# Attention softmax, gate, transposes and masks of a hybrid decoder layer: sinks as a 129th key slot, a tanh gate, turns two blocks behind, weights scaled on ScalarE, masks by affine selection

## The chip, the cores and the metric

One Trainium2 chip, one core of it. The metric is the device time of one execution of the whole program, in microseconds (us), the median of several runs. The engines are named as the profile names them: PE (TensorE matmul), PEld (its weight load), DVE (VectorE), ACT (ScalarE), POOL (GpSimd) and SP (SyncE, which issues the DMAs here). Each engine works through its own instruction list in order.

## What is computed

One decoder layer over 2048 tokens of width 1024, in float32. Batch is 1, depth is 1.

```python
hn = rms_norm(h, ln1_g); proj = hn @ w_in + b_in          # q 512 | k 128 | v 128 | u 512
q, k = partial_rotary(q), partial_rotary(k)
s = q k^T / 8 within a window of 128, 8 heads over 2 key-value heads
m = max(max(s), sink); p = exp(s - m)
attn = (p / (sum(p) + exp(sink - m))) @ v
y = gelu(s5_ssm(u, ...))                                   # tanh form of gelu
ssm = y * sigmoid(y @ w_glu + b_glu)
h = h + concat(rms_norm(attn, g_attn), rms_norm(ssm, g_ssm)) @ w_out
up = causal_conv3(rms_norm(h, ln2_g) @ w_up) + conv_b      # 2 x 2816 columns
h = h + (silu(gate) * val) @ w_down
out = rms_norm(h, lnf_g)
```

`rms_norm(x, g)` is `x * rsqrt(mean(x * x) + 1e-5) * g`.

## The kernel before

Nearly every product is made of three matmuls in the rounded format `F32R`: a number is split in a high half (a cast on ACT) and a low half (the subtraction on DVE or POOL), and high by high, high by low and low by high are summed in PSUM. The helper `split` (L133 and L115) records that. `tt_` (L115), `stt_` (L118) and `ts_` (L112) are helpers through which most elementwise work goes, so their line numbers mix many places, and the tile names tell them apart. The program runs under a scheduler that places each instruction in its engine's list and interleaves independent work, so the order of the lists is not that of the source.

The work falls into stretches of the timeline:

1. **Projection** (0 to 292 us). Blocks of 128 tokens are normalised, turned by PE, split and multiplied by `w_in`. Beside it DVE, POOL and ACT build the tables of the state space model. `rstd_of` (L119 to 129) gives the reciprocal root of a mean square: one `pow` on POOL and a Newton step on DVE.
2. **Attention beside the state space model** (292 to 616 us). `attention(b)` (L678) handles block b, for each of the two key-value heads four query heads at once: scores on PE (L695), the previous block's 128 keys copied by ACT (L699) and overwritten under a triangular mask by the block's own keys (L700), so that one tile `s` of 128 queries by 4 heads by 128 key slots holds each window. Then the maximum (L704), the negated maximum with the sink (`m`, by `stt_`), the sink's own term `e` (an addition and an exponential, L707), four exponentials with sums (L709), the sum with `e`, the reciprocal (L711) and the product of weights and reciprocal, 128x512, on DVE. PE turns the weights (L715), they are split into `th` and `tl`, POOL multiplies both by a mask into `mh` and `ml`, and PE multiplies by values (L735). `ssm(j)` runs between the blocks, and `attn_out` (L832) multiplies a finished block by the upper half of `w_out`.
3. **Gate, lower half of the output and turns** (616 to 842 us, with the start of the next). For every quarter q of 256 tokens: `d_gelu(q)` (L871) loads and applies gelu (L877); `d_gate(q)` (L883) multiplies by `w_glu` (L891) and applies the sigmoid (L893); `d_out(q, t)` (L941) multiplies a block of 128 tokens by the lower half of `w_out` (L804), adds, squares on ACT (L953) and normalises into `hn`; `d_turn(b)` (L958) turns `hn` by eight PE transposes (L965), copies them out by ACT (L966) and stores them. The loop at L1107 sets the order of these calls. ACT loads a table when the function it is to compute is not in the table it holds (ACT_TABLE_LOAD).
4. **Convolution and feed-forward** (842 us to the end): five passes of a seven-product scheme (`pair`, L1060, L1077), with elementwise work on all engines, and the final norm.

The loop that sets the order in stretch 3 is, in the kernel before:

```python
        d_out(q, 0)
        if q + 2 < NQ:
            d_gelu(q + 2)
        if q > 0:
            d_turn(q * 2 - 1)
        d_out(q, 1)
        d_turn(q * 2)
```

Of the kernel before, what the change touches and what calls it, by code (L numbers as in the profile page):

```python
# [68 lines left out]
def trunk(ctx, tc, a, out):  # L69
# [610 lines left out]
    def attention(b):  # L680
# [5 lines left out]
        for kv in range(NKV):  # L686

            s = xa.tile([P, 4, P], F32, name="u_t", bufs=4) if early else ap_.tile([P, 4, P], F32, name="s", bufs=4)
            if b == 0:
# [12 lines left out]
            e = sm.tile([P, 4], F32, name="e")  # L702
# [1 line left out]
            V.tensor_reduce(out=m, in_=s, axis=AX.X, op=ALU.max)  # L704
            stt_(m, m, -1.0, nsink[:, kv * 4:kv * 4 + 4], ALU.mult, ALU.min)
            tt_(e, sink[:, kv * 4:kv * 4 + 4], m, ALU.add)
            S.activation(out=e, in_=e, func=AF.Exp)  # L707
            for h in range(4):
                S.activation(out=s[:, h], in_=s[:, h], func=AF.Exp, bias=m[:, h:h + 1], accum_out=den[:, h:h + 1])  # L709
            tt_(den, den, e, ALU.add)  # L710
# [1 line left out]
            tt_(s, s, den.rearrange("p (h o) -> p h o", o=1).broadcast_to([P, 4, P]), ALU.mult)
# [581 lines left out]
```

## Time and profile before

| | |
|---|---|
| median of 3 runs | 2155.77 us (2153.46 to 2157.44) |
| the profiled execution, its own time | 2155.07 us |
| its span, first to last instruction | 2152.9 us |
| mean granted TensorE clock | 0.975 of full |
| PE, PEld busy | 93%, 78% of the span |
| DVE, ACT, POOL busy | 78%, 47%, 58% |

Busy time of PE is the union of matmuls that overlap in the pipeline, so a stretch in which PE is 90% busy can hold more idle issue slots than 10%. The shares over the whole span mix stretches with different limits; the section of rows below has them apart. The time outside the span (2.2 us) is the start and end of the execution.

### The profile page before, as it was taken

What the parts mean: (1) busy time and instruction counts of PE and PEld (TensorE: products, weight loads), DVE (VectorE), ACT (ScalarE), POOL (GpSimd) and SP (SyncE); (2) the same over time, 40 slices, a digit from 0 to 9 for tenths busy, and PEclk for the clock granted to TensorE, in tenths of its full rate; (3) what the DMA queues carried; (4) which work ended last, traced back from release to release, by engine and by line L of the source; (5) the groups of instructions that cost most, each with busy time, mean ns of one, the idle gap of its engine ahead of it and who ended that gap; (6) DMA issues with size and microseconds to landing.
All of it is one profiled execution on the core that took longest, in us unless ns stands there. A gap on an engine that the chain in (4) does not pass through costs nothing.

```text
span 2152.9 us, 29873 instructions
## 1 busy us (share of the span) xinstructions
PE 2003.9 (93%) x10057; PEld 1681.7 (78%) x10057; DVE 1681.9 (78%) x2778; ACT 1013.6 (47%) x2071; POOL 1238.0 (58%) x1180
## 2 busy tenths in 40 slices
PE   7999987899889988999999999999999899999986
PEld 6889976788778867888888778888887687788664
DVE  6988357999976787777777987877779967857888
ACT  5575335655546644444444554444544423323333
POOL 1656215666642355555555775454547868968864
PEclk9999987999999999999999999999999999999998
DMA  7476478677746752313233323132333545645543
GB/s 211 147 270 245 140 244 248 200 225 233 198 147 196 227 194 92 104 60 98 79 113 102 118 88 108 60 98 79 108 100 124 208 150 192 219 162 169 198 149 130
DMA packets 304622, 335.50 MB, mean 156 GB/s; under 512 B 92070, under 2 KB 237910, under 8 KB 302934
## 3 DMA queue, kind: packets, MB, share of 16 engines
q1 hardware_dynamic: 304470, 333.60, 48.2%
q8 instruction: 80, 1.31, 0.2%
q14 instruction: 72, 0.59, 0.1%
HBM read 214.14 MB, written 119.41 MB: 155 GB/s over the span
## 4 chain that ended last, share of the span: by engine, by line
PE 48%; DVE 8%; POOL 4%; issue 2%; DMA 2%; ACT 1%; DVEq 0%; ACTq 0%; POOLq 0%
PE ps L1077 17%; PE pz L1077 17%; PE pi L1077 7%; PE po L1077 6%; DMA sg<-in_w_down_dram 1%; DVE sums L115 1%; DVE yl L115 1%; DVE sg L115 1%; DVE yl L118 1%; DVE rs L118 1%; POOL xt L115 1%; POOL ln L115 1%; DVE rs L115 1%; PE pi L804 0%; PE po L804 0%
## 5 line engine op out<-in xcount | busy, mean ns | idle before, releaser
L118 DVE SCALAR_TENSOR_TENSOR pp<-yl,cw,pp 128x512 f32<-128x512 f32 x176 | 131.9, 750 | 38.5 <-ACT pp L1158 37.9
L115 POOL TENSOR_TENSOR rs<-rs,mhalf 128x1 f32<-128x1 f32 x80 | 51.6, 652 | 162.7 <-DVE rs L112 156.3
L1163 ACT ACTIVATE xh<-pp 128x512 f32<-128x512 f32 x88 | 52.7, 598 | 93.9 <-DVE pp L118 93.0
L1158 ACT ACTIVATE pp<-yl,cb,cw 128x512 f32<-128x512 f32 x88 | 69.0, 784 | 53.9 <-DVE yl L115 52.9
L115 DVE TENSOR_TENSOR yl<-pz,yl 128x512 f32<-128x512 f32 x66 | 45.3, 686 | 49.6 <-PE pz L1077 47.2
L115 POOL TENSOR_TENSOR xt<-sums,xt 128x512 fp32r<-128x512 f32 (+1 forms) x39 | 52.6, 1349 | 48.1 <-ACT xt L133 48.1
L218 PE MATMUL pz<-hnT_lo,wu_h 128*128 128x256 f32 x256 | 73.6, 290 | 2.6 <-DVE hnT_lo L115 2.6
L115 POOL TENSOR_TENSOR atl<-sums,atl 128x512 fp32r<-128x512 f32 (+1 forms) x40 | 56.2, 1404 | 33.2 <-ACT atl L133 33.1
L218 PE MATMUL pz<-hnT_hi,wu_h 128*128 128x256 f32 x256 | 71.9, 290 | 3.2 <-ACT hnT_hi L133 3.2
L115 POOL TENSOR_TENSOR ln<-sums,ln 128x512 fp32r<-128x512 f32 (+1 forms) x43 | 55.8, 1299 | 31.5 <-ACT ln L133 30.9
L218 PE MATMUL pz<-hnT_hi,wu_l 128*128 128x256 f32 x256 | 72.5, 286 | 0.0
L115 POOL TENSOR_TENSOR sq<-sums,sq 128x512 fp32r<-128x512 f32 (+1 forms) x42 | 54.7, 1303 | 27.6 <-ACT sq L133 26.0
L115 DVE TENSOR_TENSOR sums<-yt 128x512 f32<-128x512 f32 (+1 forms) x48 | 59.4, 1238 | 13.6 <-POOL ln L115 4.0
L115 POOL TENSOR_TENSOR ath<-sums,ath 128x512 fp32r<-128x512 f32 (+1 forms) x40 | 55.2, 1380 | 25.4 <-ACT ath L133 25.4
L709 ACT ACTIVATE s<-s,m 128x128 f32<-128x128 f32 x120 | 46.9, 392 | 43.2 <-DVE m L118 43.2
L115 POOL TENSOR_TENSOR sq<-sq 128x256 f32<-128x256 f32 (+1 forms) x64 | 42.7, 680 | 42.0 <-ACT sq L817 39.6
L115 POOL TENSOR_TENSOR vv<-vv 128x255 f32<-128x255 f32 x32 | 26.3, 822 | 67.6 <-DVE vv L115 62.6
L115 DVE TENSOR_TENSOR sg<-sg,sg 128x2048 f32<-128x2048 f32 (+1 forms) x20 | 51.5, 2575 | 15.5 <-DMA sg<-in_w_down_dram 11.0
L804 PE MATMUL pi<-w_oh,ath 128*128 128x512 f32 x128 | 55.0, 430 | 8.6 <-DVE rs L112 6.2
L115 DVE TENSOR_TENSOR xh<-px,xh 128x512 f32<-128x512 f32 x88 | 60.5, 687 | 1.9
L115 POOL TENSOR_TENSOR xt<-yh,xt 128x512 fp32r<-128x512 f32 (+1 forms) x28 | 41.5, 1480 | 28.5 <-ACT xt L133 28.4
L115 DVE TENSOR_TENSOR yl<-ps,yl 128x512 f32<-128x512 f32 x70 | 47.9, 685 | 11.3 <-PE ps L1077 10.0
(1261 smaller groups left out, 7966.9 us busy)
## 6 DMA issues: line engine op xcount, KB each, us to landing
xh<-h_d SPq DMA_DIRECT2D x48, 512.0 KB, 4.1
yt<-in_w_up_dram SPq DMA_DIRECT2D x44, 512.0 KB, 4.2
yh<-in_w_up_dram SPq DMA_DIRECT2D x44, 512.0 KB, 3.8
act_d<-xh SPq DMA_DIRECT2D x44, 512.0 KB, 3.3
h_d<-yl SPq DMA_DIRECT2D x32, 512.0 KB, 3.7
qk_d<-qx SPq DMA_DIRECT2D x16, 768.0 KB, 3.2
sg<-h_d SPq DMA_DIRECT2D x12, 1024.0 KB, 6.0
sg<-in_w_down_dram SPq DMA_DIRECT2D x12, 1024.0 KB, 5.7
```

Of the source, the lines that this page charges most:

```text
L115: (eng or V).tensor_tensor(out=o, in0=x, in1=y, op=op)
L118: V.scalar_tensor_tensor(out=o, in0=x, scalar=s, in1=y, op0=o0, op1=o1)
L218: E.matmul(out=pu, lhsT=l["u"][:, k, cs], rhs=r[:, k, :], start=n == 0, stop=n == 3 * KT - 1)
L709: S.activation(out=s[:, h], in_=s[:, h], func=AF.Exp, bias=m[:, h:h + 1], accum_out=den[:, h:h + 1])
L804: E.matmul(out=po, lhsT=l[:, k, :], rhs=r[k][:, cs], start=n == 0, stop=n == 11)
L1077: E.matmul(out=b, lhsT=l[:, k], rhs=r[:, k], start=m == 0, stop=m == 3 * kh - 1)
L1158: S.activation(out=v, in_=u[s_][:, o + 2:o + 2 + HF], func=AF.Identity, scale=w2, bias=cb[:, fc_:fc_ + 1])
L1163: S.activation(out=x, in_=v, func=AF.Silu)
```

## The change

- `rstd_of` takes two DVE operations behind the `pow` and not three. It gives minus two times the value, and the factor is taken back in the gains: `ln1`, `g_a`, `g_s`, `ln2` and `lnf` are scaled once when they are loaded, and `sumsq` gets a scale for the gated half.
- In `attention` for all blocks but the first, the sink is a 129th column of two fixed tiles (`slots`, one for even and one for odd blocks, each with both key-value heads), filled once by POOL. Maximum and exponentials run over 129 columns; `m`, `e`, their addition and the addition to the sum go away. The exponentials write to a tile `w`.
- The weights are multiplied by the reciprocal in four ACT operations of 128x128 (Copy with a scale per partition), not in one of DVE.
- `mh` and `ml` are made by affine selection on POOL, and not by a product with a mask.
- The gate is `tanh(x/2) + 1` times gelu, with the factors taken into `bg` and `g_s`; the multiplication becomes a `stt_`.
- `d_gelu`'s load is a function of its own, `d_load`, called a quarter earlier.
- `d_turn` runs two blocks behind `d_out`, and `hn` of every first block of a quarter stands in a `sums` tile.

```diff
@@ rstd_of
-        tt_(t, y, y, ALU.mult)
-        stt_(t, t, -0.5, v, ALU.mult, ALU.mult)
-        stt_(r, t, 1.5, y, ALU.add, ALU.mult)
+        stt_(t, y, v, y, ALU.mult, ALU.mult)
+        stt_(r, t, -3.0, y, ALU.add, ALU.mult)
@@ attention
+            else:
+                s = slots[b % 2]
...
-            V.tensor_reduce(out=m, in_=s, axis=AX.X, op=ALU.max)
-            stt_(m, m, -1.0, nsink[:, kv * 4:kv * 4 + 4], ALU.mult, ALU.min)
-            tt_(e, sink[:, kv * 4:kv * 4 + 4], m, ALU.add)
-            S.activation(out=e, in_=e, func=AF.Exp)
...
+                s = s[:, kv]
+                V.tensor_reduce(out=m, in_=s, axis=AX.X, op=ALU.max, negate=True)
+                w = ap_.tile([P, 4, P + 1], F32, name="w")
             for h in range(4):
-                S.activation(out=s[:, h], in_=s[:, h], func=AF.Exp, bias=m[:, h:h + 1], accum_out=den[:, h:h + 1])
-            tt_(den, den, e, ALU.add)
+                S.activation(out=w[:, h], in_=s[:, h], func=AF.Exp, bias=m[:, h:h + 1], accum_out=den[:, h:h + 1])
             V.reciprocal(out=den, in_=den)
-            tt_(s, s, den.rearrange("p (h o) -> p h o", o=1).broadcast_to([P, 4, P]), ALU.mult)
+                for h in range(4):
+                    S.activation(out=w[:, h, 0:P], in_=w[:, h, 0:P], func=AF.Copy, scale=den[:, h:h + 1])
...
-                tt_(mh, f(th), kb_(cc[:, C_MC:C_MC + P], 4), ALU.mult, Q)
-                tt_(ml, f(tl), kb_(cc[:, C_MC:C_MC + P], 4), ALU.mult, Q)
+                for o, i in ((mh, th), (ml, tl)):
+                    Q.affine_select(out=o, in_=i, compare_op=ALU.is_ge, fill=0.0, base=0,
+                                    pattern=[[0, 4], [1, P]], channel_multiplier=-1)
@@ d_gate
-            S.activation(out=pg, in_=pg, func=AF.Sigmoid, bias=bg[:, o:o + 1])
-            tt_(sm_[:, o].rearrange("p k t -> p t k"), yg[:, o].rearrange("p (t k) -> p t k", t=T),
-                pg.rearrange("p (t k) -> p t k", t=T), ALU.mult)
+            S.activation(out=pg, in_=pg, func=AF.Tanh, bias=bg[:, o:o + 1], scale=0.5)
+            stt_(sm_[:, o].rearrange("p k t -> p t k"), pg.rearrange("p (t k) -> p t k", t=T), 1.0,
+                 yg[:, o].rearrange("p (t k) -> p t k", t=T), ALU.add, ALU.mult)
@@ d_out
-        hn = xh()
+        hn = xh() if t else acc.tile([P, D], F32, name="sums", bufs=2)
@@ the loop over quarters
+        if q + 3 < NQ:
+            d_load(q + 3)
         d_out(q, 0)
         if q + 2 < NQ:
             d_gelu(q + 2)
         if q > 0:
+            d_turn(q * 2 - 2)
+        d_out(q, 1)
+        if q > 0:
             d_turn(q * 2 - 1)
-        d_out(q, 1)
-        d_turn(q * 2)
```

DVE's list, in the middle of the attention stretch, for about one key-value head: `zb` is the scan of the state space model, `xh` the sum of an output block, `rs` the rstd. Before, and then in the changed kernel:

```order
L704 TENSOR_REDUCE m<-s 128x4
L115 TENSOR_TENSOR ul<-u,uh 128x512
L115 TENSOR_TENSOR tl<-pp,th 128x512
L118 SCALAR_TENSOR_TENSOR m<-m,aux 128x4
L700 COPY_PREDICATED s<-cc,ps 128x256
L115 TENSOR_TENSOR e<-aux,m 128x4
L118 SCALAR_TENSOR_TENSOR xh<-pi,rs,xh 128x512
L115 TENSOR_TENSOR den<-den,e 128x4
L711 RECIPROCAL den<-den 128x4
L115 TENSOR_TENSOR s<-s,den 128x512
```

```order
L704 COPY_PREDICATED s_3991<-cc,ps 128x2x128
L118 SCALAR_TENSOR_TENSOR rs<-rs 128x1
L716 TENSOR_REDUCE m<-s_3991 128x4
L722 RECIPROCAL den<-den 128x4
L118 SCALAR_TENSOR_TENSOR xh<-pi,rs,xh 128x512
L115 TENSOR_TENSOR zl<-vv,zh 128x512
L627 SCALAR_TENSOR_TENSOR zb_3460<-rad,vv 128x255
```

Four DVE operations for each head pair are gone, three of them small and one of 128x512; between maximum and reciprocal only other work is left.

ACT's list in the same stretch, before and then changed (`u` is the output of the state space model, `th` the split of the turned weights):

```order
L699 COPY s<-ps 128x256
L709 ACTIVATE s,den<-s,m 128x128 x4
L707 ACTIVATE e<-e 128x4
L133 CAST th<-pp 128x512
L699 COPY s<-ps 128x256
```

```order
L719 ACTIVATE w,den<-s_3991,m 128x129 x4
L640 COPY u<-pz 128x256
L727 ACTIVATE w<-w,den 128x128 x4
L703 COPY s_3991<-ps 128x2x128
L132 CAST ath<-po 128x512
```

Four scalings (L727) stand behind the four exponentials, and what is behind them on ACT waits while DVE takes the reciprocal.

ACT's list in the stretch of gates and turns, before and then changed (`yt` is gelu, `pz` the gate, `xh` or `sums` the square of an output block, `xt` the copies of a turn):

```order
L953 ACTIVATE xh,ss<-yl 128x1024
L877 ACT_TABLE_LOAD
L877 ACTIVATE yt<-yt 128x1024
L893 ACT_TABLE_LOAD
L893 ACTIVATE pz<-pz,bg 128x256
L966 COPY xt<-pp 128x512
L966 COPY xt<-px 128x512
```

```order
L986 ACTIVATE xh,ss<-yl 128x1024
L922 ACTIVATE pz<-pz,bg 128x256 x2
L906 ACTIVATE yt<-yt 128x1024
L922 ACTIVATE pz<-pz,bg 128x256
L132 CAST yh<-yt 128x1024
L922 ACTIVATE pz<-pz,bg 128x256
L999 COPY xt<-pp 128x512
```

The table loads around gelu and gate are gone: the whole program has 16 before and 5 now, two of the five in front of a gelu and one of them in front of an exponential of the last blocks.

## Rows read from the trace of the kernel before

**Rows 1.** Windows: length, then busy (count) PE PEld DVE ACT POOL, PEclk, DMA, GB/s.

```profile
292.00:360.00 68.00, 46.36 (x242) 40.42 (x241) 53.44 (x106) 35.03 (x89) 28.47 (x26) 0.75 0.85 262
360.00:616.00 256.00, 230.21 (x1502) 206.03 (x1502) 237.68 (x492) 148.04 (x471) 161.17 (x152) 0.96 0.68 206
616.00:700.00 84.00, 81.34 (x498) 71.76 (x497) 55.81 (x118) 48.97 (x76) 21.39 (x34) 1.00 0.65 189
700.00:842.00 142.00, 122.99 (x628) 103.44 (x627) 102.26 (x169) 73.13 (x117) 68.94 (x68) 0.94 0.60 188
842.00:2130.00 1288.00, 1245.68 (x5342) 1006.59 (x5341) 1014.88 (x1326) 546.20 (x896) 823.32 (x672) 0.99 0.38 125
```

**Rows 2.** The chain (start, length, work), then PE's timeline: matmuls 512 and 256 wide.

```profile
869.68 2.80 PE ps L1077 x12
...
690.20 0.28 PE L891 MATMUL pz<-yh,uwl 128*128 128x256 f32 x1
690.32 0.40 PE L891 MATMUL pz<-yh,uwh 128*128 128x256 f32 x2
690.55 0.28 PE L891 MATMUL pz<-yh,uwl 128*128 128x256 f32 x1
```

**Rows 3.** Windows of L804 alone, PE and PEld: its 512-wide matmuls in 360 to 616.

```profile
360.00:616.00 256.00, 89.74 (x338) 65.59 (x338) 0.96 0.68 206
```

**Rows 4.** Waits of PE, 616 to 842: us, times, longest; then a window of 8 us.

```profile
PE pp L965 <- DVE xh L118: 10.7, 4, 5.4
...
PE pp L965 <- DVE rs L118: 2.2, 1, 2.2
PE pz L891 <- DVE sm__9239 L115: 2.2, 1, 2.2
...
756.00:764.00 8.00, 5.82 (x26) 5.09 (x25) 7.96 (x8) 2.56 (x5) 4.76 (x3) 0.57 0.36 126
```

**Rows 5.** Groups of DVE, 360 to 616: count, busy, mean ns, idle before.

```profile
L115 DVE TENSOR_TENSOR s<-s,den 128x512 f32<-128x512 f32 x28 | 26.4, 942 | 0.1
...
L115 DVE TENSOR_TENSOR den<-den,e 128x4 f32<-128x4 f32 x28 | 13.2, 473 | 3.0 <-ACT e L707 2.5 <-ACT s L709 0.4
L115 DVE TENSOR_TENSOR e<-aux,m 128x4 f32<-128x4 f32 x28 | 12.1, 431 | 0.1
L118 DVE SCALAR_TENSOR_TENSOR m<-m,aux 128x4 f32<-128x4 f32 x28 | 10.2, 365 | 0.0
...
L115 DVE TENSOR_TENSOR rs<-rs 128x1 f32<-128x1 f32 x14 | 5.8, 412 | 0.5 <-POOL rs L115 0.4
```

**Rows 6.** L115 on DVE in 360 to 616: ns min/median/max; then the timeline.

```profile
L115 DVE TENSOR_TENSOR e<-aux,m x28: 127/162/1247, 362.9 to 596.1; 128x4 f32<-128x4 f32 x28
...
L115 DVE TENSOR_TENSOR s<-s,den x28: 660/688/1771, 367.2 to 598.8; 128x512 f32<-128x512 f32 x28
...
341.50 2.35 POOL L115 TENSOR_TENSOR w_ol<-xh,w_oh 128x1024 fp32r<-128x1024 f32 x1
...
341.82 2.05 DVE L115 TENSOR_TENSOR e<-aux,m 128x4 f32<-128x4 f32 x1
```

**Rows 7.** Groups of ACT by form, 90 to 180: scale per partition, 128x128.

```profile
L513 ACT ACTIVATE tt<-tb,php 128x128 f32<-128x128 f32 x16 | 6.3, 396 | 4.3 <-DVE tb L118 4.1
```

**Rows 8.** POOL: the masks of 360 to 616; a cast of one input (ns min/median/max).

```profile
L115 POOL TENSOR_TENSOR mh<-th,cc 128x512 fp32r<-128x512 f32 x29 | 40.3, 1388 | 25.0 <-ACT th L133 24.9
...
L169 POOL CAST wu_h<-u_t x1: 697/697/697, 11.1 to 11.1; 128x512 fp32r<-128x512 f32 x1
```

**Rows 9.** Groups of ACT, 616 to 842: table loads; then one in the timeline.

```profile
L893 ACT ACT_TABLE_LOAD x7 | 9.0, 1283 | 0.1
L877 ACT ACT_TABLE_LOAD x6 | 7.7, 1283 | 14.3 <-DMA yt<-ys_d 14.3
...
839.93 1.28 ACT L1163 ACT_TABLE_LOAD   x1
841.23 0.60 ACT L1163 ACTIVATE xh<-pp 128x512 f32<-128x512 f32 x1
```

More of the change, by code (lines that the diff above doesn't have):

```diff
@@ L177, in trunk @@
     Y.dma_start(out=ln1, in_=a["ln1_g"][0].rearrange("(k p) -> p k", p=P))
+    S.mul(out=ln1, in_=ln1, mul=-0.5)
     load_w("u", 0)
@@ L686, in attention @@
         for kv in range(NKV):
-            s = xa.tile([P, 4, P], F32, name="u_t", bufs=4) if early else ap_.tile([P, 4, P], F32, name="s", bufs=4)
-            if b == 0:
+            if early:
+                s = xa.tile([P, 4, P], F32, name="u_t", bufs=4)
                 V.memset(s, NEG)
+            else:
+                s = slots[b % 2]
             for r in range(2):
@@ L701, in attention @@
             m = sm.tile([P, 4], F32, name="m")
[L702 removed]
             den = sm.tile([P, 4], F32, name="den")
[L704 to L707 removed]
+            if early:
+                e = sm.tile([P, 4], F32, name="e")
+                V.tensor_reduce(out=m, in_=s, axis=AX.X, op=ALU.max)
+                stt_(m, m, -1.0, nsink[:, kv * 4:kv * 4 + 4], ALU.mult, ALU.min)
+                tt_(e, sink[:, kv * 4:kv * 4 + 4], m, ALU.add)
+                S.activation(out=e, in_=e, func=AF.Exp)
+                w = s
+            else:
+                s = s[:, kv]
+                V.tensor_reduce(out=m, in_=s, axis=AX.X, op=ALU.max, negate=True)
+                w = ap_.tile([P, 4, P + 1], F32, name="w")
             for h in range(4):
[L709 to L710 removed]
+                S.activation(out=w[:, h], in_=s[:, h], func=AF.Exp, bias=m[:, h:h + 1], accum_out=den[:, h:h + 1])
+            if early:
+                tt_(den, den, e, ALU.add)
             V.reciprocal(out=den, in_=den)
[L712 removed]
+            if early:
+                tt_(s, s, den.rearrange("p (h o) -> p h o", o=1).broadcast_to([P, 4, P]), ALU.mult)
+            else:
+                for h in range(4):
+                    S.activation(out=w[:, h, 0:P], in_=w[:, h, 0:P], func=AF.Copy, scale=den[:, h:h + 1])
+            s = w[:, :, 0:P]
             pt = bank("pp", [P, 4, P])
@@ L790, in next_v @@
         load_v(b, vpad[b % 3], vpad[3 + b % 2] if b > 0 else None)
+    slots = [ap_.tile([P, NKV, 4, P + 1], F32, name=f"s{i}", bufs=1) for i in range(2)]
+    for t in slots:
+        Q.tensor_copy(out=t[:, :, :, P], in_=sink.rearrange("p (v h) -> p v h", v=NKV))
     idrs[0] = ap_.tile([P, P], F32R, name="idr", bufs=1)
@@ L812, in xt, with sumsq @@
         return oa.tile(shape or [P, D], F32, name="xt", bufs=1)
-    def sumsq(t):
+    def sumsq(t, scale=1.0):
         sq = oa.tile([P, 4, P], F32, name="sq")
-        S.activation(out=sq, in_=t, func=AF.Square)
+        S.activation(out=sq, in_=t, func=AF.Square, scale=scale)
         tt_(sq[:, 0:2], sq[:, 0:2], sq[:, 2:4], ALU.add, Q)
@@ L849, in load_gate @@
         Y.dma_start(out=bg, in_=a["b_glu"][0].rearrange("(k p) -> p k", p=P))
+        ts_(g_s, g_s, -0.25, ALU.mult)
+        ts_(bg, bg, 0.5, ALU.mult)
         wg, wsh, wsl = ([], []), [], []
@@ L869, in trunk, with d_load @@
     ygs, hns = {}, {}
+    yts = {}
+    def d_load(q):
+        k0 = q * 256 // T
+        yts[q] = gy.tile([P, 4, T, 32], F32, name="yt")
+        for j in range(4):
+            Y.dma_start(out=yts[q][:, j], in_=ys_d[j * P:(j + 1) * P, :, k0:k0 + 32])
     def d_gelu(q):
-        k0 = q * 256 // T
-        yt = gy.tile([P, 4, T, 32], F32, name="yt")
-        for j in range(4):
-            Y.dma_start(out=yt[:, j], in_=ys_d[j * P:(j + 1) * P, :, k0:k0 + 32])
+        yt = yts.pop(q)
         yg = yt.rearrange("p j t k -> p j (t k)")
@@ L916, in trunk @@
         if b == NB - 1:
+            for q in range(2):
+                d_load(q)
             d_gelu(0)
@@ L919, in trunk @@
             d_gelu(1)
+            d_load(2)
         if b not in ats:
@@ L938, in trunk @@
     Y.dma_start(out=ln2, in_=bcast(a["ln2_g"][0], D))
+    S.mul(out=ln2, in_=ln2, mul=-0.5)
     def d_out(q, t):
@@ L1123, in trunk @@
                 res.append(next(b0))
-    d_turn(NB - 1)
+    for b in (NB - 2, NB - 1):
+        d_turn(b)
     gws.close()
@@ L1252, in trunk @@
             Y.dma_start(out=lnf, in_=bcast(a["lnf_g"], D))
+            S.mul(out=lnf, in_=lnf, mul=-0.5)
         def dn_pair(q, w):
```

5 lines of the change are left out of this document (3 added, 2 removed).

## The prediction

> **What bounds the kernel now.** I read the windows first, because the shares of the whole span mix stretches with different limits. In 842 to 2130 us PE is busy 1245.7 of 1288 us [rows 1]: the feed-forward part is PE's, and the change puts nothing into it but a scale of a gain at a load. What the change touches lies before it. In 360 to 616 the row says DVE 237.7 of 256 us (93%) beside PE 230.2, POOL 161.2 and ACT 148.0 [rows 1]. DVE is the fullest, and PE's busy time flatters PE, since matmuls overlap. So I count what PE needs: 12 matmuls 512 wide take 2.80 us, 0.233 each, and the starts of the 256-wide ones show three in 0.35 us, 0.117 each [rows 2]. Of the 1502 matmuls of the stretch 338 are of the output product, 512 wide [rows 3], and I take all others at 0.117 (the narrower ones are no dearer by much). That is 338 x 0.233 + 1164 x 0.117 = 79 + 136 = 215 us. PE has 41 us to give in this stretch, and DVE 18.
>
> In 616 to 700 PE is at 81.3 of 84 us, in 700 to 842 at 123.0 of 142 [rows 1], and there its waits name the cause: 10.7 and 2.2 us before the first transpose of a turn (L965), for `hn` from DVE, and 2.2 before a gate's matmul [rows 4]. From 292 to 360 the DMA engines are at 0.85 and the granted clock is 0.75 [rows 1]: a ramp that waits for loads.
>
> **The change part by part.** All sums are against the profiled execution, 2155.07 us; the median of the runs shown is 0.7 above it.
>
> *DVE in the attention stretch.* Gone are the product with the reciprocal (26.4 us in 28), the sum of the denominator (13.2), the sink's addition (12.1) and the negated maximum (10.2): 61.9 us. One operation of `rstd_of` goes too, 14 times 0.412, 5.8 us [rows 5]. That is 67.7 by the means. The medians are far under the means: 0.688 us for the product, and 0.16 for the 128x4 addition that has a mean of 0.43 and a longest of 1.25 [rows 6]. The timeline shows why: such an addition starts 0.3 us into a POOL product of 2.35 us and ends with it, 2.05 us later [rows 6]. By medians the removal is worth 28 x (0.688 + 3 x 0.16) + 14 x 0.16 = 35 us, and what lies between, 33 us, is waiting for POOL, which may pass to the operations that stay. So DVE falls from 237.7 to between 170 and 203 us. Both are below the 215 that PE needs: DVE stops being the bound, and PE's matmul list is next.
>
> The Trainium skill ("SBUF — State Buffer", section "SBUF: two separate sides") says that a DVE operation with two SBUF inputs and a GpSimd operation that reads SBUF exclude each other for the whole instruction. The trace agrees [rows 6], and by that rule affine selection, which reads SBUF, still blocks DVE: it would keep DVE at the upper of the two figures, as in the first rival below.
>
> *ACT.* 28 x 4 = 112 scalings come in. A scale per partition of 128x128 takes 0.396 us [rows 7], 44 us together; at nothing, if they only fill idle time, the lower end is 0. ACT goes from 148 to at most 192 us, 83% of the stretch that I forecast. They stand behind the exponentials, and what follows on ACT waits for the reciprocal; it is no bound yet, but close enough to be a rival.
>
> *POOL.* 59 masks at 1.388 us are 82 us of 161 [rows 8]. No row shows affine selection. The nearest is a cast with one input and 128x512 elements, 0.697 us [rows 8]; the far end is the two-input price, no gain; a dearer one can't be excluded and is a rival. I take 0.9, nearer to the cast, as one operand is read: POOL 133 us, not the bound either way. The two fills of the sink column hide in the ramp.
>
> *The sum of the stretch.* Today PE's 215 us stand in 256, 0.84. In 616 to 700, where PE is fed by dense products, its busy share is 0.97 [rows 1]. With DVE relieved but with the same in-order chains I take 0.93: 215 / 0.93 = 231, **25 us less**. Ends: 8 (0.87) and 40 (PE full).
>
> *Gates and turns.* Two blocks behind, a turn has another block's 24 output matmuls (24 x 0.233 = 5.6 us) more between `hn` and its transposes; the longest wait was 5.4 [rows 4]. So I take the 12.9 us as gone. What is late next is the last block's turn, which stands before feed-forward matmuls in both orders and is no worse. The table loads: 13 become 2 in this stretch, 11 x 1.28 = 14.1 us off ACT [rows 9]. ACT has room there (49.0 of 84 and 73.1 of 142 [rows 1]), so only the gate's wait, 2.2 us, is what this can shorten on PE; I take 2. The multiplication becomes a `stt_`, and the rstd loses 32 small operations at 0.16 to 0.41 us, 5 to 13 us of DVE: cover for the former. After the idle time of 756 to 764 (PE 5.8 of 8 us) the granted clock stands at 0.57, between its levels of 1.2 and 2.4 GHz [rows 4]; without the idle I give 3 us back of it, from the 0.43 x 8 = 3.4 that the window lost. New costs: `d_load` puts four issues ahead of the next block's `h_d` load on SP, and `hn` of even blocks waits for a `sums` tile; 2 us. Sum: 12.9 + 2 + 3 - 2 = **16 us less**, ends 3 and 27.
>
> The Trainium skill ("ScalarE: Activation LUTs", section "What ACT_TABLE_LOAD costs") gives a load a drain of about 1.38 us beside its 1.28. The trace differs: the next ACT operation starts 0.02 us after the load [rows 9]. By the page the 11 loads would be 29 us of ACT; as ACT is not the bound there, the sum would be lower by 2 us at most.
>
> *The rest.* Projection: PE's chain through `rstd_of` is shorter by one operation of 0.16 us for each of 16 blocks, most of it hidden behind the matmuls of another pair, and the scale of `ln1` stands before the first weights: 1 us less. Feed-forward: POOL's list is word for word the same and PE's nearly; 0, with 4 either way for its boundaries. The last norm loses two small operations: 0.3. **Together 25 + 16 + 1.3 = 42 us**; 2155.07 - 42 = 2113, and 2114 for the median.
>
> **The rivals.**
> 1. *DVE's waits for POOL move to the operations that stay*, and selection is as long as the product. For it: the 33 us are waits, and half of POOL's time is not the masks. Against: POOL may get shorter. DVE stays at 203 us beside PE's 215; both nearly full need some 245: 11 us, not 25. 2128.
> 2. *ACT becomes the bound of the attention stretch.* Its list now holds exponentials, a DVE round trip and scalings of each head pair. At 192 us and half a microsecond of waiting for each of the 28 reciprocals more, 206, it fills 0.83 of 248: 8 us and not 25. 2131. Against: ACT is at 148 of 256 us now [rows 1], and its exponentials get their maximum two DVE operations earlier.
> 3. *The turns' wait only moves*, to `sums` or to the loads behind `d_load`, and the last turn delays the feed-forward part: 3 us and not 16. 2127.
> 4. *PE full in both stretches*: 40 + 27 + 2. 2087.
> 5. *Slower: affine selection is dear.* POOL has 161 - 82 = 79 us of other work in the stretch, so it becomes the bound from (256 - 79) / 59 = 3.0 us for each. At 5 us the stretch is 79 + 295 = 374, 118 longer, and with the 17 gained elsewhere the kernel takes 2256; at 4.0, 2197. Against: the product of two operands takes 1.388 us, its waits included [rows 8].
>
> That the change doesn't do what it says can't be: the lists show it.
>
> **How the numbers follow.** Forecast, 2104 to 2122: 0.42. Rivals: 0.20, 0.13, 0.09, 0.10 and 0.06. The range, 2084 to 2137, reaches over the forecast and rivals 1, 3 and most of 2 and 4; it leaves out the fifth and the ends of 2 and 4, under 0.2. What a measurement can tell from no change is about 0.2%, 4.3 us. All cases but the fifth, and a tail of the second and third together, are faster by more: faster 0.91, same 0.03, slower 0.06.
>
> **What would show it.** Right: the attention stretch (first score to last value product) about 25 us shorter, DVE's busy share there at most 0.85, PE's waits for `hn` before L965's successor under 2 us, two table loads in the gates, affine selections near 0.7 to 1 us, the feed-forward part as long as before. Wrong: long means of the small DVE operations that stay (rival 1), scalings that end ACT's lists late and PE waiting for turned weights (rival 2), PE waiting at the start of the feed-forward part (3), POOL above 0.9 in the stretch (5).

## The result, and the profile after

The changed kernel takes **2130.63 us** (median of 4 runs, 2130.52 to 2135.21), beside 2154.61 (2153.02 to 2157.44) for the kernel before: a ratio of 0.9886, 95% interval 0.9874 to 0.9899, 24 us less. The forecast was 2114, 42 us less, in a range of 2084 to 2137. The direction and the first term held; the second term did not. The time lies outside the forecast's own 2104 to 2122 and inside the range, which reached so far because it took in the rivals. The profiled execution of the changed kernel is its slowest (2135.21 us, span 2133.5).

To see where the time was gained, I compare the times at which both kernels have done the same amount of matmul work. The work is each kernel's matmuls by shape, 0.233 us for 512 wide and 0.117 for 256 wide [rows 2], 0.11 for 128 wide (four in 0.44 us in a turn). A column says by how much the kernel is behind the one before (minus: ahead) where that one stands at the given time; e1 to e12 are the experiments below. An entry is good to some 2 us, as the way of counting moves single entries by that much.

| time before, us | after | e1 | e2 | e5 | e6 | e9 | e10 | e12 |
|---|---|---|---|---|---|---|---|---|
| 340 | +2.9 | +3.6 | +0.9 | +1.8 | +1.8 | +1.0 | -0.8 | +1.1 |
| 460 | -7.3 | +0.8 | -11.7 | -2.7 | +4.8 | -9.1 | -16.5 | -18.7 |
| 620 | -18.8 | -1.4 | -23.6 | -13.3 | +5.3 | -20.6 | -32.9 | -30.4 |
| 700 | -20.2 | +0.7 | -22.3 | -9.6 | +9.7 | -22.1 | -31.1 | -29.9 |
| 840 | -18.2 | +3.1 | -18.8 | -7.4 | +12.1 | -25.5 | -29.5 | -33.2 |
| 1000 | -18.8 | +3.1 | -19.4 | -7.6 | +12.3 | -26.1 | -29.9 | -33.8 |

One of e1's ten executions took 6507 us at a granted clock of 0.30; its median has that one in it, its ratio has not.

All of the gain comes between 340 and 620 us: 18.8 + 2.9 = 22 us there. From 620 to 1000, through gates, turns and the start of the feed-forward part, nothing is added. Most of the 2.9 us at the start is no cost of the change: in this execution ACT got the first weights at 8.6 us, and at 6.8 in that of the kernel before, and over all runs the first transpose starts anywhere from 8.9 to 11.1 us with the old reciprocal root and from 9.7 to 11.0 with the new one.

The windows, first a stretch of the kernel before that the rows ahead do not have, for later comparison (columns as in [rows 1]):

```profile
345.00:575.00 230.00, 204.55 (x1341) 184.00 (x1341) 215.53 (x452) 133.40 (x433) 140.85 (x132) 0.94 0.70 214
```

and the windows of the changed kernel:

```profile
345.00:575.00 230.00, 215.31 (x1473) 196.21 (x1472) 184.62 (x372) 174.46 (x549) 122.62 (x150) 0.97 0.78 236
...
605.00:681.00 76.00, 74.38 (x447) 65.19 (x445) 45.79 (x96) 37.56 (x64) 21.05 (x33) 1.00 0.59 166
681.00:823.00 142.00, 123.14 (x617) 102.76 (x616) 101.42 (x140) 66.01 (x110) 68.21 (x65) 0.92 0.61 186
823.00:2110.00 1287.00, 1247.23 (x5345) 1008.27 (x5344) 1021.93 (x1315) 545.88 (x895) 822.54 (x672) 0.99 0.38 125
```

In the same 230 us of attention PE does 1473 matmuls and not 1341. DVE falls from 0.94 to 0.80 of the time, ACT rises from 0.58 to 0.76, POOL falls. PE stands at 0.94: DVE is no longer the fullest engine. The stretch of the last gates, 681 to 823, is the old one over again: 123.1 of 142 us for PE, 101.4 for DVE, 68.2 for POOL, against 123.0, 102.3 and 68.9 [rows 1]. Groups of the changed kernel in 345 to 575 us:

```profile
L115 DVE TENSOR_TENSOR zl<-vv,zh 128x512 fp32r<-128x512 f32 x26 | 21.2, 815 | 6.7 <-ACT zh L132 6.5
...
L118 DVE SCALAR_TENSOR_TENSOR rs<-rs 128x1 f32<-128x1 f32 x26 | 11.7, 452 | 2.9 <-POOL rs L115 2.7
L115 DVE TENSOR_TENSOR ul<-u,uh 128x512 fp32r<-128x512 f32 x12 | 9.7, 806 | 4.9 <-ACT uh L132 4.9
...
L722 DVE RECIPROCAL den<-den 128x4 f32<-128x4 f32 x28 | 4.8, 171 | 6.2 <-ACT w L719 5.9
...
L746 POOL TENSOR_SCALAR_AFFINE_SELECT mh<-th 128x512 fp32r<-128x512 f32 x27 | 19.3, 717 | 23.4 <-ACT th L132 22.8 <-DMA ms<-m_d 0.5
...
L727 ACT ACTIVATE w<-w,den 128x128 f32<-128x128 f32 x112 | 36.6, 400 | 2.4 <-DVE den L722 2.4
```

Affine selection takes 0.72 us where the product took 1.39 [rows 8], so POOL is no bound. The scalings cost 0.400 us, as forecast from 0.396 [rows 7]. DVE's idle time now ends at ACT: 6.5 us for `zh`, 4.9 for `uh`, 5.9 for the exponentials of `w`. The waits of PE, 605 to 823 us, in the place of [rows 4]:

```profile
PE pi L825 <- DVE yl L118: 9.3, 2, 5.4
PE ps L1110 <- POOL sq L115: 5.0, 1, 5.0
PE pp L998 <- ACT xt L999: 2.1, 2, 1.6
```

The waits for `hn` are gone, as forecast. In their place PE waits for the eviction of an output bank (`yl`) and, at the start of the feed-forward part, for POOL. The sum has hardly moved: all waits of PE that this view names come to 20.4 us here, and to 21.5 in the same view of the kernel before (616 to 842 us). The timeline of DVE, POOL and PE around the longest of them (start, length):

```profile
726.06 2.29 DVE L115 TENSOR_TENSOR sg<-sg,sg 128x2048 f32<-128x2048 f32 x1 [5.74 <-DMA sg<-h_d]
...
730.48 4.70 POOL L115 TENSOR_TENSOR r1l<-sg,r1h 128x1024 fp32r<-128x1024 f32 x2
730.49 5.40 DVE L118 SCALAR_TENSOR_TENSOR rs<-rs 128x1 f32<-128x1 f32 x4
735.81 1.82 DVE L118 SCALAR_TENSOR_TENSOR sums<-yl,rs,ln 128x1024 f32<-128x1024 f32 x1
737.55 0.74 DVE L118 SCALAR_TENSOR_TENSOR yl<-pi,rs,yl 128x512 f32<-128x512 f32 x1
738.44 0.77 PE L825 MATMUL pi<-dwh,ath 128*128 128x512 f32 x1 [5.41 <-DVE yl L118]
739.00 0.63 PE L825 MATMUL pi<-dwl,ath 128*128 128x512 f32 x1
739.43 0.63 PE L825 MATMUL pi<-dwh,atl 128*128 128x512 f32 x1
```

`r1l` is a low half of the feed-forward's first operand, which `fixed` already prepares here, with its subtractions on POOL. Two of them run from 730.48 to 735.18, and for as long four DVE operations of 128x1 stand still (e9 shows three of them in 0.40 us). Behind them wait the norm of `sums`, then the eviction, then PE, 5.4 us. After that the 512-wide matmuls start 0.43 us apart and not 0.23, and the windows of that wait and of what follows it show why (the column before DMA is the granted clock):

```profile
733.00:738.40 5.40, 0.03 (x1) 0.00 (x0) 5.40 (x6) 1.43 (x3) 5.36 (x5) 0.91 0.68 208
738.40:744.20 5.80, 5.76 (x16) 4.52 (x16) 4.52 (x5) 3.06 (x5) 1.77 (x2) 0.50 0.97 244
744.20:750.00 5.80, 5.80 (x40) 5.32 (x39) 3.46 (x6) 1.09 (x3) 3.75 (x4) 0.99 0.58 216
```

PE does nothing for 5.4 us, and for the next 5.8 the clock is granted at 0.50, its lower level of 1.2 GHz. Twelve 512-wide matmuls start there 0.43 us apart: 12 x 0.2 = 2.4 us lost on top of the wait. It is the collision of [rows 6], at a place where the prediction did not look.

The second wait, 5.0 us at the start of the feed-forward part, has the same cause. DVE and POOL each make two low halves at once, the norm of the last block (`rs`) comes behind them, and the `sq` that PE waits for stands behind that norm in POOL's list:

```profile
784.73 5.63 POOL L115 TENSOR_TENSOR r4l<-sg,r4h 128x1024 fp32r<-128x1024 f32 x2
788.06 4.51 DVE L115 TENSOR_TENSOR r6l<-sg,r6h 128x1024 fp32r<-128x1024 f32 x2
792.78 0.55 POOL L115 TENSOR_TENSOR rs<-rs,mhalf 128x1 f32<-128x1 f32 x1 [2.42 <-DVE rs L112]
793.30 1.26 POOL L115 TENSOR_TENSOR sq<-sums,sq 128x512 fp32r<-128x512 f32 x1
794.62 1.22 PE L1110 MATMUL ps<-r2h,sq 128*128 128x512 f32 x2 [4.98 <-POOL sq L115]
```

The kernel before has the same subtractions ahead of its longest wait for `hn`, 5.4 us, which is that of the last block's turn:

```profile
802.96 5.73 POOL L115 TENSOR_TENSOR r4l<-sg,r4h 128x1024 fp32r<-128x1024 f32 x2
803.61 6.16 DVE L115 TENSOR_TENSOR r6l<-sg,r6h 128x1024 fp32r<-128x1024 f32 x2 [2.23 <-ACT r6h L133]
814.65 1.09 PE L965 MATMUL pp<-cc,xh 128*128 128x128 f32 x4 [5.43 <-DVE xh L118]
```

### The profile page after: what moved, and what is told of

The parts are those of the page before. It is cut to its first block, busy times and chain, and to the rows that moved or that the text cites. A ratio compares the mean times of both kernels' runs of the same rounds, so it can differ in the third digit from the quotient of the medians.

```text
span 2133.5 us, 29682 instructions
## 1 busy us (share of the span) xinstructions
PE 1999.6 (94%) x10057; PEld 1680.3 (79%) x10057; DVE 1622.5 (76%) x2581; ACT 1031.4 (48%) x2153; POOL 1199.0 (56%) x1182
## 4 chain that ended last, share of the span: by engine, by line
PE 53%; DVE 9%; DMA 5%; POOL 4%; issue 3%; ACT 1%; SPq 0%; POOLq 0%; DVEq 0%; ACTq 0%
PE ps L1110 17%; PE pz L1110 17%; PE pi L1110 7%; PE po L1110 7%; PE pi L825 2%; DMA sg<-in_w_down_dram 1%; DVE sums L115 1%; PE po L825 1%; DVE rs L118 1%; DMA sg<-h_d 1%; PE pz L920 1%; DVE sg L115 1%; DVE yl L118 1%; DVE yl L115 1%; POOL xt L115 1%
## 5 line engine op out<-in xcount | busy, mean ns | idle before, releaser
L115 POOL TENSOR_TENSOR rs<-rs,mhalf 128x1 f32<-128x1 f32 x80 | 50.8, 640 | 181.8 <-DVE rs L112 179.1
L1195 ACT ACTIVATE pp<-yl,cb,cw 128x512 f32<-128x512 f32 x88 | 68.9, 783 | 53.4 <-DVE yl L115 52.3
L118 DVE SCALAR_TENSOR_TENSOR rs<-rs 128x1 f32<-128x1 f32 x160 | 66.6, 420 | 20.0 <-POOL rs L115 18.0
L115 DVE TENSOR_TENSOR yl<-pz,yl 128x512 f32<-128x512 f32 x66 | 45.3, 686 | 45.9 <-PE pz L1110 43.3
L115 POOL TENSOR_TENSOR xt<-sums,xt 128x512 fp32r<-128x512 f32 (+1 forms) x39 | 51.7, 1325 | 48.6 <-ACT xt L132 48.6
L115 POOL TENSOR_TENSOR ln<-sums,ln 128x512 fp32r<-128x512 f32 (+1 forms) x43 | 56.8, 1322 | 32.3 <-ACT ln L132 32.1
L115 POOL TENSOR_TENSOR atl<-sums,atl 128x512 fp32r<-128x512 f32 (+1 forms) x40 | 56.2, 1406 | 32.5 <-ACT atl L132 32.5
L115 POOL TENSOR_TENSOR sq<-sq 128x256 f32<-128x256 f32 (+1 forms) x64 | 45.7, 729 | 43.2 <-ACT sq L838 42.4
L115 POOL TENSOR_TENSOR ath<-sums,ath 128x512 fp32r<-128x512 f32 (+1 forms) x40 | 55.6, 1389 | 25.1 <-ACT ath L132 23.2
L115 POOL TENSOR_TENSOR vv<-vv 128x255 f32<-128x255 f32 x32 | 26.5, 828 | 75.3 <-DVE vv L115 72.0
L115 DVE TENSOR_TENSOR sums<-yt 128x512 f32<-128x512 f32 (+1 forms) x48 | 60.0, 1249 | 11.1 <-POOL xt L115 3.1
L115 DVE TENSOR_TENSOR sg<-sg,sg 128x2048 f32<-128x2048 f32 (+1 forms) x20 | 51.3, 2565 | 20.5 <-DMA sg<-in_w_down_dram 11.4
L115 POOL TENSOR_TENSOR sq<-sums,sq 128x512 fp32r<-128x512 f32 (+1 forms) x42 | 54.2, 1291 | 20.6 <-ACT sq L132 17.2
L115 DVE TENSOR_TENSOR xh<-px,xh 128x512 f32<-128x512 f32 x88 | 60.5, 688 | 1.9
L115 POOL TENSOR_TENSOR xt<-yh,xt 128x512 fp32r<-128x512 f32 (+1 forms) x28 | 41.4, 1480 | 27.4 <-ACT xt L132 27.4
L239 PE MATMUL pi<-wq_h,hnT_hi 128*128 128x512 f32 x128 | 52.1, 407 | 4.9 <-DVE qf L118 3.6
```

What stands on the lines that cost most here:

```text
L115: (eng or V).tensor_tensor(out=o, in0=x, in1=y, op=op)
L118: V.scalar_tensor_tensor(out=o, in0=x, scalar=s, in1=y, op0=o0, op1=o1)
L239: E.matmul(out=pq, lhsT=l[:, k, ts], rhs=r["q"][:, k, 0:512], start=st, stop=sp_)
L1195: S.activation(out=v, in_=u[s_][:, o + 2:o + 2 + HF], func=AF.Identity, scale=w2, bias=cb[:, fc_:fc_ + 1])
```

## The experiments

Twelve kernels ran. The program's lists of instructions are laid out anew for each (the scheduler interleaves the work), so most variants differ from their parent in more than the edit. How much is said where it matters. Ratios are to the kernel before, in runs on the same chip.

**e1, gates and turns alone.** The kernel before with `d_load`, the tanh gate, the new order of turns and `hn` in `sums`, the reciprocal root left as it was:

```diff
-            S.activation(out=pg, in_=pg, func=AF.Sigmoid, bias=bg[:, o:o + 1])
+            S.activation(out=pg, in_=pg, func=AF.Tanh, bias=bg[:, o:o + 1], scale=0.5)
...
+            d_turn(q * 2 - 2)
+        d_out(q, 1)
+        if q > 0:
             d_turn(q * 2 - 1)
-        d_out(q, 1)
-        d_turn(q * 2)
```

> The kernel before, with the gate and turn part alone (tanh gate, loads of the scan's rows ahead, turns two blocks behind); attention, masks and reciprocal root as before. Theory A (the two parts add up, each with its own stretch): gates and turns give about half of the 24 us, so 2140 to 2146 us, with the stretch up to attention's last output product as long as before and the one behind it 10 to 14 us shorter. Theory B (the gain is one chain: gates could only start early because attention let them): the gate part alone gives under 4 us, 2150 us or more. Theory C (the gate part carries the whole gain): 2132 us or less.

2156.55 us, 0.9996 (0.9986 to 1.0005): nothing. That is within what theory B says of this run, though most of the waits for `hn` are gone; the next run speaks against B. Its waits of PE from 616 to 845 us begin

```profile
PE ps L824 <- POOL sq L115: 7.0, 3, 5.4
PE ps L1087 <- POOL sq L115: 5.0, 1, 5.0
PE pp L975 <- DVE rs L118: 2.6, 1, 2.6
```

where 12.9 us for `hn` stood before [rows 4]; 2.6 of them are left. 12.0 us now end at POOL, and all waits that the view names come to 20.5 us, beside 21.5 before. The same subtractions stand ahead of these waits: at the longest of them POOL itself is busy with two of `r1l`, 5.71 us, before it comes to what PE waits for.

**e2, attention alone.** The kernel before with all of the change that stands in `attention`:

```diff
+                s = slots[b % 2]
...
+                V.tensor_reduce(out=m, in_=s, axis=AX.X, op=ALU.max, negate=True)
...
+                    S.activation(out=w[:, h, 0:P], in_=w[:, h, 0:P], func=AF.Copy, scale=den[:, h:h + 1])
...
+                    Q.affine_select(out=o, in_=i, compare_op=ALU.is_ge, fill=0.0, base=0, ...)
```

> The kernel before, with the attention part alone (sink as a 129th slot, ScalarE scales, affine selection masks); gates, turns and reciprocal root as before. Theory A: the other half, 2140 to 2146 us, and VectorE's busy share of the attention stretch at 0.80 as in the changed kernel. Theory B: 2150 us or more. Theory C: within 3 us of the kernel before.

2137.49 us, 0.9906 (0.9882 to 0.9929): 20 us, more than half; the interval reaches to that of the whole change. The attention part carries nearly all of the result, and its column in the table above shows the gain in its own stretch. B and C fall, and of A the halves. Against e2, whose gates are the old ones, the changed kernel is better by 0.0020, 4 us, which the intervals do not part. Whether the gates, turns and reciprocal root are worth that much beside the attention part stays open.

**e3, masks by product, and e4, scaling on VectorE.** Both from the changed kernel:

```diff
-                    Q.affine_select(out=o, in_=i, compare_op=ALU.is_ge, fill=0.0, base=0, ...)
+                tt_(mh, f(th), kb_(cc[:, C_MC:C_MC + P], 4), ALU.mult, Q)
+                tt_(ml, f(tl), kb_(cc[:, C_MC:C_MC + P], 4), ALU.mult, Q)
```

> The changed kernel with GpSimd's mask products in place of the affine selections. If GpSimd's length, or VectorE's wait behind it, mattered: 5 to 8 us slower than the changed kernel (2136 to 2139 us), VectorE's small operations in the attention stretch longer. If GpSimd had slack: within 2 us of 2130.6.

2132.74 us, 0.9885 (0.9868 to 0.9902): as the changed kernel. Rival 1's mechanism shows all the same. The group of small DVE operations that stay, 345 to 575 us, means 452 ns in the changed kernel and here

```profile
L118 DVE SCALAR_TENSOR_TENSOR rs<-rs 128x1 f32<-128x1 f32 x28 | 20.7, 740 | 1.4 <-POOL rs L115 1.3
```

and DVE's busy time rises from 184.6 to 197.1 of 230 us. It costs no time that shows, with DVE filled to 0.86.

```diff
-                for h in range(4):
-                    S.activation(out=w[:, h, 0:P], in_=w[:, h, 0:P], func=AF.Copy, scale=den[:, h:h + 1])
+            tt_(w[:, :, 0:P], w[:, :, 0:P], den.rearrange(...).broadcast_to([P, 4, P]), ALU.mult)
```

> The changed kernel with the weights scaled by one VectorE product for each key head again instead of four ScalarE instructions; sink slot and affine selection stay. If VectorE still sets the attention stretch: 26 us of work comes back to it and 8 to 15 us of time (2139 to 2146 us). If TensorE, its clock or ScalarE sets it now: within 3 us of 2130.6.

2126.85 us, 0.9863 (0.9841 to 0.9885): not slower, and 3.8 us under the changed kernel, which the intervals don't part. What was the largest single item of the forecast, 26.4 us of DVE [rows 5], can go back to DVE at no loss, as long as slot and selection stay. DVE's busy share alone does not tell the bound. It is back at 0.92 here, and PE does more matmuls than in the changed kernel:

```profile
345.00:575.00 230.00, 216.50 (x1500) 197.35 (x1499) 212.62 (x405) 145.29 (x453) 128.99 (x152) 0.99 0.78 236
```

**e5, the slot alone; e6, its buffers alone; e7, scaling alone.** From the kernel before. e5 takes the sink slot and nothing else; e6 has scores and exponentials in tiles of their own, without the slot; e7 only puts the four scalings in the place of the product.

```diff
+                s = slots[b % 2]
...
+            tt_(w[:, :, 0:P], w[:, :, 0:P], den.rearrange(...).broadcast_to([P, 4, P]), ALU.mult)
```

> The kernel before with the sink as a 129th key slot and nothing else: the weights are still scaled by one VectorE product, the masks are still GpSimd products, gates and reciprocal root as before. Theory S (the slot carries the gain: it takes four small VectorE instructions and one ScalarE exponential out of the chain of each softmax): 2128 to 2138 us. Theory V (VectorE's load carries it, so that slot and scaling must both go): 2143 us or more. The slot brings more buffers with it (scores and weights in tiles of their own); the next run has these alone.

2148.39 us, 0.9967 (0.9954 to 0.9980): 7 us. The slot alone, with the tiles that it brings, is not the gain, and S misses, though it takes away the three small operations, 35.5 of the 61.9 us that the prediction counted by means [rows 5]. By V the scaling would have to go too; e10 says otherwise.

```diff
-            s = xa.tile(...) if early else ap_.tile([P, 4, P], F32, name="s", bufs=4)
+            s = xa.tile(...) if early else slots[b % 2][:, kv]
...
+            w = s if early else ap_.tile([P, 4, P], F32, name="w")
```

> The kernel before with scores and exponentials in tiles of their own (four tiles of scores, two of weights, as in the changed kernel) and no sink slot; every instruction stays. If the buffers carry the gain: 2130 to 2140 us. If the shorter chain of the sink slot carries it: within 4 us of the kernel before.

2168.12 us, 1.0068 (1.0053 to 1.0083): 14 us slower. Neither theory has it. Every instruction is the same, but where tiles come free differs, and so the lists: by the shortest edit that turns one list into the other, some 1,300 of PE's 10,057 matmuls are taken out or put in. Of the 10.5 us that it falls behind from 340 to 1000 us (table), 7 arise after 620, in stretches which the edit does not touch. Whether the two tiles of weights or the new order costs this stays open. If it is the order, differences of 10 us between kernels whose lists differ prove little singly, those of e5 and e7 among them. If it is the tiles, e5 has to be set beside e6, which has as many tiles without the slot: then the slot is worth 0.0101, 22 us, and theory S was right about the size.

```diff
-            tt_(s, s, den.rearrange(...).broadcast_to([P, 4, P]), ALU.mult)
+                for h in range(4):
+                    S.activation(out=s[:, h], in_=s[:, h], func=AF.Copy, scale=den[:, h:h + 1])
```

> The kernel before with the weights scaled in place by four ScalarE instructions instead of the VectorE product, and nothing else. Theory V (the forecast's: VectorE's load sets the attention stretch, so 26 us less of it give 8 us or more): 2147 us or less. Theory S (the chain of a softmax sets it; four scalings of 0.40 us take longer than one product of 0.94): within 4 us of the kernel before, or slower.

2144.36 us, 0.9955 (0.9941 to 0.9970): 10 us. It comes out as theory V says for the kernel before: with DVE at 0.94, 26 us less of it are worth 10, within the doubt that e6 leaves.

**e8, the old reciprocal root** in the changed kernel, with the gains' factors taken back:

```diff
-        stt_(t, y, v, y, ALU.mult, ALU.mult)
-        stt_(r, t, -3.0, y, ALU.add, ALU.mult)
+        tt_(t, y, y, ALU.mult)
+        stt_(t, t, -0.5, v, ALU.mult, ALU.mult)
+        stt_(r, t, 1.5, y, ALU.add, ALU.mult)
...
-    S.mul(out=ln1, in_=ln1, mul=-0.5)
```

> The changed kernel with the old reciprocal root (one more VectorE instruction of 128x1 in each, no halving of the gains beforehand). If the new root saves only its 80 or so instructions of 0.06 to 0.3 us: within 3 us of 2130.6. If the scaling of the first gain, ahead of the weights on ScalarE, delays the start of the projection as the profile of the changed kernel could be read: 2 to 4 us faster, its first transpose at 9.2 us instead of 11.0.

2133.06 us, 0.9895 (0.9872 to 0.9918): no difference. Its first transpose is at 10.8 us, as late as in the changed kernel: the gain's scaling at the start delays nothing.

**e9, residues on VectorE.** The changed kernel, one string changed, so that DVE and not POOL makes the low halves of the feed-forward's first operand:

```diff
-    b0 = fixed(h2_load(0), 4, "VQQQQVV")
+    b0 = fixed(h2_load(0), 4, "VVVVVVV")
```

> The changed kernel with the four residue subtractions of the feed-forward's first operand that GpSimd does during the last gates (128x1024, 2.4 to 2.8 us each) done by VectorE. Theory G (GpSimd's long subtractions hold VectorE's small operations, 5.4 us for four of 128x1, and with them the output banks' evictions, so that the turns' gain is lost): TensorE's wait for yl (9.3 us) and for sq (5.0 us) in the second half of the gates falls under 3 us in sum, and the kernel gains 4 to 10 us. Rival (VectorE is full there and the work only moves): within 3 us of the changed kernel, or slower.

2127.23 us, 0.9858 (0.9843 to 0.9874), beside 0.9886 (0.9874 to 0.9899): 0.0028, some 6 us by the ratios. By the medians themselves it is 3.4 us, as the kernel before took 2158.17 beside these runs and 2154.61 beside those of the changed kernel; the gain lies between. The lists are nearly the same: some 90 of PE's 10,057 matmuls are taken out or put in. The waits of PE from 605 to 823 us:

```profile
PE ps L1110 <- ACT sq L132: 3.0, 1, 3.0
PE ps L1110 <- POOL sq L115: 2.4, 1, 2.4
PE ps L845 <- POOL sq L115: 2.1, 1, 2.1
PE pp L998 <- DVE sums L118: 2.0, 1, 2.0
PE pp L998 <- DVE xh L118: 1.4, 2, 1.1
```

`yl` is gone from the list. The waits for `sq` at the start of the feed-forward part stay nearly as long: 5.4 us (3.0 for ACT and 2.4 for POOL), where they were 5.9 (0.9 and 5.0). So the sum that theory G wanted under 3 us is 5.4 at the least, down from 14.3 with `yl`, and 3.4 us for `hn` are back. All waits that the view names come to 14.0 us, beside 20.4 in the changed kernel: 6.4 less. DVE at the place of the long wait:

```profile
727.80 0.40 DVE L118 SCALAR_TENSOR_TENSOR rs<-rs 128x1 f32<-128x1 f32 x3
728.11 1.22 DVE L115 TENSOR_TENSOR r1l<-sg,r1h 128x1024 fp32r<-128x1024 f32 x1
729.25 0.15 DVE L118 SCALAR_TENSOR_TENSOR rs<-rs 128x1 f32<-128x1 f32 x1
```

Three small operations take 0.40 us, and the fourth 0.15, where the four took 5.40, and the subtraction takes 1.22 us on DVE where POOL needs 2.35. DVE gets more work and is free earlier. In the table, e9 keeps within 2 us of the changed kernel up to 700 us and gains from there. That is theory G at the first of its two places, in the cause and in the size of the gain; the second is nearly as slow as it was.

**e10, slot and selection.** e5 with the masks by selection; the product stays on DVE.

```diff
-                tt_(mh, f(th), kb_(cc[:, C_MC:C_MC + P], 4), ALU.mult, Q)
-                tt_(ml, f(tl), kb_(cc[:, C_MC:C_MC + P], 4), ALU.mult, Q)
+                for o, i in ((mh, th), (ml, tl)):
+                    Q.affine_select(out=o, in_=i, compare_op=ALU.is_ge, fill=0.0, base=0, ...)
```

> The kernel before with the sink slot and the affine selection, the weights still scaled by VectorE; gates and reciprocal root as before. It differs from the run of the slot alone (2148.4 us, 0.9967) by the selection only. Theory P (GpSimd's products hold VectorE's operations on two operands; without them VectorE needs no relief by ScalarE): 2128 to 2138 us, VectorE's product at 0.85 us or less and its waits gone. Theory N (the selection is worth nothing, as the run of the changed kernel with mask products says): 2143 to 2150 us; the good time of the changed kernel with scaling on VectorE then came from the gates or from another order of the work.

2128.52 us, 0.9865 (0.9852 to 0.9879): the time is that of theory P. Two of the change's edits do all that the whole does. Against e5 it differs by the selection, and by 0.0102, 22 us; in the window of 345 to 575 us, first e5,

```profile
345.00:575.00 230.00, 209.94 (x1402) 189.18 (x1402) 207.60 (x391) 136.26 (x423) 156.66 (x139) 0.96 0.75 228
```

then e10:

```profile
345.00:575.00 230.00, 216.22 (x1490) 194.98 (x1489) 212.80 (x420) 149.24 (x454) 129.14 (x153) 1.00 0.79 237
```

DVE's price per matmul of PE falls from 207.60/1402 = 0.148 us to 212.80/1490 = 0.143 (0.161 before, 0.125 in the changed kernel). At the same fill that is 3.5%, some 9 us of 256. The other 13 are DVE's fill (0.90 to 0.93), the granted clock (0.96 to 1.00) and the order of the lists, which I cannot part. DVE's waits for POOL are not gone, as theory P has it, but shorter: the product takes 0.846 us on average, where it has 0.906 in e5 and 0.66 at the least [rows 6]. From the groups of e10 in the same window:

```profile
L115 DVE TENSOR_TENSOR w<-w,den 128x512 f32<-128x512 f32 x29 | 24.5, 846 | 0.5
...
L115 DVE TENSOR_TENSOR zl<-vv,zh 128x512 fp32r<-128x512 f32 x26 | 22.8, 875 | 0.6 <-ACT zh L133 0.6
...
L721 DVE RECIPROCAL den<-den 128x4 f32<-128x4 f32 x29 | 4.9, 170 | 5.6 <-ACT w L718 5.5
```

Against e2 e10 is better by 0.0041, 9 us, and e4 against the changed kernel points the same way: with slot and selection in place, scaling on ACT seems to cost. With lists that differ and differences of this size it is not settled.

**e11, four tiles of weights** in e4:

```diff
-                w = ap_.tile([P, 4, P + 1], F32, name="w")
+                w = ap_.tile([P, 4, P + 1], F32, name="w", bufs=4)
```

> The changed kernel with scaling on VectorE and four tiles of weights instead of two. If the two tiles, held from the exponential to the transposes, delay the next softmax: 3 to 8 us faster than the run with scaling on VectorE (2126.9, 0.9863). If TensorE is as full as it gets in the attention stretch (0.94 busy): within 3 us of it.

2125.23 us, 0.9846 (0.9830 to 0.9862), beside e4's 0.9863 (0.9841 to 0.9885): no difference that can be told. The instruction lists of all engines are the same in both, so this pair has no new order in it; its 0.0017 also shows by how much two kernels with the same lists may differ. That speaks against the two tiles as the cause of e6's loss, though e6 was not run with four.

**e12, together:** the edits of e4, e9 and e11.

> The changed kernel with three edits together: weights scaled by VectorE, four tiles of weights, and the residues of the feed-forward's first operand on VectorE. If the gains lie in different stretches (attention: 0.9846 with the first two, gates: 0.9858 against 0.9886 with the third) they add: 2116 to 2122 us. If the gates' stretch is full once the attention stretch ends earlier: 2124 to 2128 us.

**2119.25 us**, 0.9828 (0.9814 to 0.9841): 37 us under the kernel before and some 11 under the changed one, and what addition gives (0.9846 - 0.0028 = 0.9818) lies within its interval.

## Why the prediction was right, and where its sum failed

- **What bounds the attention stretch: right.** DVE at 0.93 was the bound. The sign held, DVE's share is 0.80 (forecast: at most 0.85). PE does 1473 matmuls where it did 1341, 1.10 times as many; the forecast's fill of 0.93 for 0.84 is 1.11 times.
- **The attention term, 25 us: right**, 22 measured in the profiled execution. It was right as a sum, and less so as a reason. DVE's load had more than one cure. Slot alone (e5) gains 7 us and scaling alone (e7) 10. Slot with scaling (e3, with the new gates) gains 25 and slot with selection (e10) 29, where all three give 20 (e2) and 24 (the changed kernel): a second cure is worth more than the first, and a third nothing. No run has the selection alone, or selection with scaling. The point is that the bound moves. As soon as DVE has room, a further relief buys nothing (e3), and the 112 scalings are work on the engine that DVE then waits for: 6.5 us for `zh` in the changed kernel, 0.6 in e10, whose scaling is DVE's. The 5.9 for the exponentials are not the scalings' doing, as e10 has 5.5. Rival 2 had that mechanism at an ACT filled to 83%; ACT was at 76%, and e10 against e2 is the 9 us that it may have cost. What bounds the stretch after the change no run shows; in e2, e4 and e10 to e12 PE is 0.94 to 0.95 busy.
- **The gate and turn term, 16 us: wrong; it measured 0** (table, 620 to 1000 us; e1). Of its parts, "12.9 us as gone" is where the sum failed. The waits for `hn` did go, but the step looked only at who is waited for and not at why `hn` was late. DVE's list was held by the long subtractions for the feed-forward part, on POOL and on DVE itself, before the change as after it, and whatever came next in the lists took over the wait: of 21.5 us of waits in all, 20.4 are left. The step also counts as gone the 5.4 us that were the last block's own wait, though of that turn it says only that it is no worse. e9 takes part of the cause away, and 3 to 6 us of the term appear. The clock's 3 us did not come back for the same reason: the idle time moved, and the clock fell behind it (0.92 from 681 to 823 us, 0.94 before). The 2 us of table loads were cover only: 16 loads became 5, one of them among the gates (at 609.5 us) where the forecast had two, and e1, which has 3, gains nothing.
- **Rival 3** named the right outcome, "the wait only moves", and 2127. Of its places `sums` and the loads behind `d_load` were wrong, and the eviction it did not name. Its sign, PE waiting at the start of the feed-forward part, came true with 5.0 us, behind the last block's norm.
- **The range held by its width.** Rivals 1, 2 and 3 had 2128, 2131 and 2127, the measured 2130.63 is among them, and the cause of the miss is the third's.
- **Affine selection: 0.9 us taken, 0.72 measured** (0.64 median). Rival 5's 3.0 us are four times that.
- **Projection -1, feed-forward 0:** nothing to be seen of either; e8 has the root at no effect. The feed-forward row has 1247.2 us of PE in 1287, as before.

Without the failed term the forecast is 25 + 0 + 1.3 = 26 us, and the medians are 24 apart.

## What to carry to other kernels

When a wait on an engine is to be removed, ask what held that engine's list, not which operation was named last: if the holder stays, the next consumer inherits the wait. Add up all the waits before and after: a sum that stays says that the wait has only moved. Edits that relieve the same bound need not add up; try each alone and undo each alone, for the one that moves work to the next fullest engine may give nothing or cost. Here two subtractions on POOL, 4.70 us, cost through what they held on DVE, four operations that took 5.40 us in place of 0.55.
